# Moving the sums of the next weights, one weight buffer and twenty subtractions in a two-layer encoder trunk

## The chip, the cores and the metric

The kernel runs on one core of a Trainium2 chip. The metric is the device time of one execution in microseconds (us); the time before is the median of 3 runs, 2132.06 us (2131.26 to 2143.67). A core has TensorE for matrix products, VectorE, ScalarE and GpSimd for elementwise work, and a queue on SyncE (SP) that issues the transfers. Each engine works through its own instructions in order; they wait for one another through semaphores.

## The reference, cut to what matters

Two layers, each made of a feed-forward block, a mixer (dilated attention beside an mLSTM) and a second feed-forward block, each between two RMS norms. x is 512 tokens by 1024. The change touches the first half of the feed-forward block alone, four times in the program:

```python
def swiglu(h, w_in, w_out):
    gu = h @ w_in                      # 512 x 1024 times 1024 x 5632
    g, u = jnp.split(gu, 2, axis=-1)   # gate and up, 2816 columns each
    return (jax.nn.silu(g) * u) @ w_out
```

## The kernel before, in words

**Products.** Weights and activations are float32, but each product is made of three passes over rounded parts: a high part `hi` (a cast on ScalarE) and a low part `lo` (the source minus `hi`, a subtraction). TensorE runs hi by hi, hi by low and low by hi (`product`, L242 to L248: 12 matmuls of 256 columns for half of the 1024 rows).

**Blocks of the feed-forward input.** `ffn_in` (L252) cuts the 2816 gate columns, and the up columns with them, into 22 blocks f of 128. The first five, the **opening**, are made plainly (`block`, L273): for the left 256 tokens, then for the right 256. Each loads gate and up weights (512 KB each) into a ring of three buffers `raw`, casts `hi` (L97) and subtracts `lo` (L98). In the five left blocks the gate's `lo` is made on VectorE and the up's on GpSimd (`G if pool and gu`). While the left blocks run, the norm, transposes and splits of the last two token tiles are still being made (`post`, `pre`, `put`); the small power in `rsqrt_sum` (L135) runs on GpSimd, the rest on VectorE and ScalarE. In the first feed-forward block these are the first instructions of the program, and `first_gain` spreads the first norm's gain through a small product.

**The other 17 blocks** (`seven`, L333) use a scheme of seven products in place of eight for the two token halves and two row halves. Besides the gate weights g and up weights u it needs four sums of their halves, made by four VectorE additions (`Weights.sums`, L311 to L314) into `ws`, and their casts and low parts (L288, L290). A block's weights are prepared while the block before it runs: inside `seven`, the calls on `nxt` are written between the products. The order on TensorE, VectorE and ScalarE in there is the order of writing (`manual_schedule`); elsewhere the framework's scheduler sets it. The gate of the left tokens is the product `pa` copied (L343) plus the product `pb`, added on VectorE (L345), passed through silu on ScalarE (L348); then ScalarE copies `pa` out (L353), and TensorE may write `pa` again (the third use of that bank in the block).

**Buffers.** The gate weights of a block are loaded into the ring of three. The up weights go to `wu`, one of two buffers (slots 17 and 19 of `chunk`): block 5 in slot 19, block 6 in slot 17, and so on by turns. The same two slots hold `xf`, the float copy of the activations from which the scheme's combinations are made; the last reading of slot 17 is `xx.finish()` (L219, L220), just ahead of the 17 blocks. The transfers are issued on SP in an order that the scheduler sets.

Of the kernel before, what the change touches and what calls it, by code (L numbers as in the profile page):

```python
# [15 lines left out]
ALU = mybir.AluOpType  # L16
# [5 lines left out]
D = 1024  # L22
# [19 lines left out]
def trunk_kernel(ctx, tc, x, norm_gain, ffn_w_in, ffn_w_out, mix_w_in, conv_w, conv_b,  # L42
                 gate_bias, mlstm_norm_gain, mix_w_out, cst, out):
    nc = tc.nc
    V, A, G, PE = nc.vector, nc.scalar, nc.gpsimd, nc.tensor
# [19 lines left out]
    def chunk(name, slot, dt=F32):  # L65
        return big.tile([P, CH], dt, tag=f"slot{slot}", name=name, bufs=1)
# [17 lines left out]
    def t2(name, slot, dt=F32):  # L84
        return tp.tile([P, 516], dt, tag=f"t{slot}", name=name, bufs=1)
# [5 lines left out]
    def raw_tile():  # L91
        return wp.tile([P, 1056], F32, tag="raw", name="raw", bufs=3)

    def halves_of(src, n, sub=None):
        hi = wp.tile([P, 1056], F32R, tag="hi", name="hi", bufs=3)
        lo = wp.tile([P, 1056], F32R, tag="lo", name="lo", bufs=3)
        A.copy(hi[:, :n], src)  # L97
        (sub or V).tensor_tensor(lo[:, :n], src, hi[:, :n].bitcast(F32), ALU.subtract)  # L98
        return [[w[:, q: q + 512].rearrange("p (k c) -> p k c", k=4) for w in (hi, lo)] for q in range(0, n, 512)]
# [49 lines left out]
    def first_gain(g):  # L149
        row, one_row = chunk("row", 20)[0:1, :D], chunk("row", 21)[0:1, :P]  # L150
        nc.sync.dma_start(row, norm_gain[0, 0:1])
        G.memset(one_row, 1.0)
        for n in range(2):
            c = slice(n * 512, n * 512 + 512)
            ps = psB("gain")
            PE.matmul(ps, one_row, row[:, c], start=True, stop=True)
            A.mul(g[:, c], ps, math.sqrt(D))

    def post(t, banks, y):
        ss = small("post_ss", 2)  # L160
# [27 lines left out]
    def fp(ap):  # L188
        return ap.bitcast(F32)
# [62 lines left out]
    def ffn_in(layer, j, xx, late=None):  # L252
        w = ffn_w_in[layer, j].rearrange("(k p) c -> p k c", p=P)
        hts = [None] * NF
        left, right, both = slice(0, 256), slice(256, 512), slice(0, 512)
        sums = [0]

        def load(f, gu, pieces=1, whole_f=False):
            raw = chunk("wu", 17 + 2 * (f % 2)) if gu and not whole_f else raw_tile()
            col = gu * FF + f * P  # L260
            dst = raw[:, :1024].rearrange("p (k c) -> p k c", k=NK)
            for k in range(0, NK, NK // pieces):
                nc.sync.dma_start(dst[:, k: k + NK // pieces], w[:, k: k + NK // pieces, col: col + P])
            return raw

        def h_of(f):
            if f % 2 == 0:
                hts[f] = chunk("ht", f // 2)
                hts[f + 1] = hts[f][:, 512:1024]
                hts[f] = hts[f][:, 0:512]  # L270
            return hts[f]

        def block(f, c, pool=False, pieces=1):  # L273
            h = h_of(f) if hts[f] is None else hts[f]
            banks = []
            for gu in range(2):
                lo_k, hi_k = halves_of(load(f, gu, pieces, True)[:, :1024], 1024, G if pool and gu else None)
                ps = psA("gu")[:, c]
                for q, w2 in enumerate((lo_k, hi_k)):
                    product(ps, w2, [x[:, 4 * q: 4 * q + 4, c] for x in (xx.h, xx.l)], q == 0)  # L280
                banks.append(ps)
            sil = t2("sil", f % 2)[:, c]
            A.activation(sil, banks[0], AF.Silu)
            V.tensor_tensor(h[:, c], banks[1], sil, ALU.mult)

        def cast_pair(hi, lo, src):

            A.copy(hi, src)  # L288
            yield
            V.tensor_tensor(lo, src, fp(hi), ALU.subtract)  # L290
            yield [[x[:, q: q + 512].rearrange("p (k c) -> p k c", k=4) for x in (hi, lo)]
                   for q in range(0, src.shape[1], 512)]

        def ring():
            return [wp.tile([P, 1056], F32R, tag=q, name=q, bufs=3)[:, :1024] for q in ("hi", "lo")]

        class Weights:


            def __init__(self, f):  # L300
                self.g, self.u = load(f, 0), load(f, 1)

            def sums(self):
                out = []
                for q in range(2):
                    out.append(chunk("ws", (18, 20, 21)[sums[0] % 3])[:, :1024])
                    sums[0] += 1
                self.s12, self.s34 = out
                s1, s2, s3, s4 = [o[:, q: q + 512] for o in out for q in (0, 512)]
                g1, g2, u1, u2 = [w[:, q: q + 512] for w in (self.g, self.u) for q in (0, 512)]  # L310
                V.tensor_tensor(s1, u1, u2, ALU.add)  # L311
                V.tensor_tensor(s3, g1, u1, ALU.subtract)
                V.tensor_tensor(s2, s1, g1, ALU.subtract)
                V.tensor_tensor(s4, g2, s2, ALU.subtract)  # L314

            def raw(self):
                self.a = cast_pair(*ring(), self.g[:, :1024])
                next(self.a)

            def one(self):  # L320
                self.one_ = cast_pair(*ring(), self.s12)
                next(self.one_)

            def two(self):
                self.two_ = cast_pair(*ring(), self.s34)
                next(self.two_)

            def last(self):
                w = one.tile([P, D], F32R, tag="nt", name="a22", bufs=2)
                self.last_ = cast_pair(w[:, :512], w[:, 512:1024], self.u[:, 512:1024])  # L330
                next(self.last_)

        def seven(f, w, nxt):  # L333
            h = h_of(f) if hts[f] is None else hts[f]
            ps = (ps_even, ps_odd)[f % 2]
            ta, tb, tc_ = [t2(q, 3 * (f % 2) + n) for n, q in enumerate(("ha", "hb", "hc"))]
            a, b, c = [ps(q)[:, :256] for q in ("pa", "pb", "pc")]
            sil0, s1, u2, s5, g1, u1 = h[:, left], ta[:, left], ta[:, right], tb[:, left], tb[:, right], tc_[:, left]
            if nxt:
                nxt.sums()  # L340
            a11, a12 = w.a
            product(a, a11, xx.b11, True)
            A.copy(s1, a)  # L343
            product(b, a12, xx.b21, True)
            V.tensor_tensor(sil0, s1, b, ALU.add)  # L345
            if nxt:
                nxt.raw()
            A.activation(sil0, sil0, AF.Silu)  # L348
            if nxt:
                nxt.a = next(nxt.a)  # L350
            w1, w2 = w.one_
            product(a, w2, xx.t[2], False)
            A.copy(u2, a)  # L353
            product(c, w1, xx.t[1], True)
            if nxt:
                nxt.one()
            A.copy(s5, c)
            if nxt:
                nxt.last()
                nxt.one_ = next(nxt.one_)  # L360
            w3, w4 = w.two_
            product(a, w3, xx.t[3], False)
            V.tensor_tensor(u1, s5, a, ALU.add)
            if nxt:
                nxt.last_ = next(nxt.last_)
            product(c, w4, xx.b22, False)
            V.tensor_tensor(g1, u2, c, ALU.add)
            if nxt:
                nxt.two()
            A.activation(g1, g1, AF.Silu)  # L370
            if nxt:
                nxt.two_ = next(nxt.two_)
            product(a, w.last_[0], xx.t[4], False)
            V.tensor_tensor(h[:, left], a, sil0, ALU.mult)
            V.tensor_tensor(h[:, right], u1, g1, ALU.mult)

        ne = 5
        for f in range(ne):
            block(f, left, True, 2 if late and f == 0 else 1)
            if late and f < 2:  # L380
                late[f]()
        for f in range(ne):
            block(f, right)
        xx.finish()
        now = Weights(ne)
        now.sums()
        for q in (now.raw, now.one, now.two, now.last):
            q()
        now.a, now.one_, now.two_, now.last_ = [next(q) for q in (now.a, now.one_, now.two_, now.last_)]
        with tc.manual_schedule(engines={mybir.EngineType.PE, mybir.EngineType.DVE, mybir.EngineType.Activation}):  # L390
            for f in range(ne, NF):
                nxt = Weights(f + 1) if f + 1 < NF else None
                seven(f, now, nxt)
                now = nxt
        return hts
# [536 lines left out]
    late = [lambda: start(2), lambda: start(3)]  # L932
    for layer in range(DEPTH):
        for sub in range(3):
# [4 lines left out]
            else:  # L939
                halves = ffn_out(layer, sub // 2, ffn_in(layer, sub // 2, xx, late), last)  # L940
                late = None
# [52 lines left out]
```

## Time and profile before

| | |
|---|---|
| median of 3 runs | 2132.06 us |
| profiled execution, time | 2134.65 us |
| profiled execution, span | 2132.9 us |
| TensorE busy in the span | 2069.2 us (97%) |
| VectorE, ScalarE, GpSimd busy | 1532.7, 1135.7, 313.4 us |
| mean granted clock of TensorE | 0.992 |

The profiled execution took 2134.65 us, 1.8 us more than its span and 2.6 us more than the median of the runs. A sum made against it is carried over to the median by its difference. TensorE is busy nearly throughout, so the time is the clean length of its instructions and the gaps between them; the places to look at are the gaps, what ended each, and stretches in which the clock was lower.

### The profile page before, as it was taken

Reading aid. Unit: us, or ns where it says so; the run is one execution under the profiler, and the core shown is the slowest. Engines: PE = TensorE matmul, PEld = TensorE weight load, DVE = VectorE, ACT = ScalarE, POOL = GpSimd, SP = SyncE. Lnnn points to the kernel's source line nnn. Section 1 sums busy time; section 2 is a strip of 40 time slices with the busy share of each in tenths; the row PEclk is TensorE's granted clock in tenths of the full one; section 3 lists DMA queues with packets and bytes.
Section 4 is the critical chain, followed back from the end, with each engine's and each line's share of the span. In section 5 each row is a group of like instructions: output and inputs, shape, how many; then the busy total and the mean of one; then the engine's idle time right before and its main releaser. Section 6 shows DMA issues by size and latency. Waiting matters only on the chain.

```text
span 2132.9 us, 35684 instructions
## 1 busy us (share of the span) xinstructions
PE 2069.2 (97%) x13918; PEld 1859.1 (87%) x13918; DVE 1532.7 (72%) x2572; ACT 1135.7 (53%) x2036; POOL 313.4 (15%) x358
## 2 busy tenths in 40 slices
PE   7999999999999999999999999999999999999998
PEld 6999988889976899998899999888898679999886
DVE  6688757785666878875787886667756568788665
ACT  5455546545565645555654555554455555455554
POOL 3000001433522300000030000014334122000000
PEclk9999999999999999999999999999999999999999
DMA  6533355541112653335565333554411236433364
GB/s 190 165 106 107 101 185 189 156 118 54 59 51 89 188 158 100 102 99 187 186 188 149 100 105 122 188 187 139 119 40 41 75 122 177 123 109 109 113 206 147
DMA packets 305887, 274.49 MB, mean 129 GB/s; under 512 B 8789, under 2 KB 275509, under 8 KB 305718
## 3 DMA queue, kind: packets, MB, share of 16 engines
q1 hardware_dynamic: 305718, 272.21, 42.5%
q8 instruction: 109, 1.79, 0.4%
q14 instruction: 60, 0.49, 0.1%
HBM read 270.08 MB, written 2.10 MB: 128 GB/s over the span
## 4 chain that ended last, share of the span: by engine, by line
PE 84%; DVE 8%; DMA 3%; issue 3%; ACT 2%; POOL 0%; SPq 0%; DVEq 0%; POOLq 0%; ACTq 0%
PE o L409 9%; PE o L412 9%; PE o L410 9%; PE pa L246 6%; PE pa L247 6%; PE pa L248 6%; PE pc L246 3%; PE pc L248 3%; PE pc L247 3%; PE nat L493 3%; PE nat L494 3%; PE nat L495 3%; PE po L887 2%; PE pb L247 1%; PE pb L248 1%
## 5 line engine op out<-in xcount | busy, mean ns | idle before, releaser
L114 DVE TENSOR_TENSOR lo<-raw,hi 128x1024 fp32r<-128x1024 f32 (+1 forms) x272 | 338.0, 1243 | 228.0 <-ACT hi L113 227.5
L113 ACT CAST hi<-raw 128x1024 fp32r<-128x1024 f32 (+1 forms) x280 | 294.7, 1053 | 321.9 <-PE o L412 226.9
L290 DVE TENSOR_TENSOR lo<-ws,hi 128x1024 fp32r<-128x1024 f32 x136 | 166.6, 1225 | 111.6 <-ACT hi L288 111.6
L410 PE MATMUL o<-lo,hq 128*128 128x512 f32 x704 | 236.9, 394 | 0.8 <-DVE lo L114 0.8
L412 PE MATMUL o<-hi,hq 128*128 128x512 f32 x704 | 223.3, 394 | 0.0
L409 PE MATMUL o<-hi,hq 128*128 128x512 f32 x704 | 210.5, 395 | 2.5 <-ACT hq L446 2.5
L288 ACT CAST hi<-ws 128x1024 fp32r<-128x1024 f32 x136 | 142.9, 1051 | 123.3 <-PE pc L247 114.8
L493 PE MATMUL nat<-hi,xh 128*128 128x256 f32 (+1 forms) x640 | 187.2, 294 | 0.0
L248 PE MATMUL gu<-xh,lo 128*128 128x256 f32 x640 | 181.7, 286 | 4.3 <-DVE lo L98 3.7
L494 PE MATMUL nat<-lo,xh 128*128 128x256 f32 (+1 forms) x640 | 182.7, 286 | 2.5 <-DVE lo L114 2.3
L247 PE MATMUL gu<-xl,hi 128*128 128x256 f32 x640 | 181.8, 285 | 2.7 <-DVE xl L201 2.7
L246 PE MATMUL gu<-xh,hi 128*128 128x256 f32 x640 | 182.0, 286 | 0.4 <-ACT hi L97 0.4
L495 PE MATMUL nat<-hi,xl 128*128 128x256 f32 (+1 forms) x640 | 182.3, 286 | 0.0
L246 PE MATMUL pa<-tq,hi 128*128 128x256 f32 x544 | 154.4, 284 | 14.5 <-ACT ha L353 14.5
L409 PEld LDWEIGHTS o<-hi,hq 128*128 128x128 f32 x704 | 131.9, 188 | 34.0 <-ACT hq L446 3.4
L246 PE MATMUL pc<-xh,hi 128*128 128x256 f32 x544 | 160.5, 295 | 0.0
L410 PEld LDWEIGHTS o<-lo,hq 128*128 128x128 f32 x704 | 131.9, 188 | 31.4 <-DVE lo L114 1.1
L412 PEld LDWEIGHTS o<-hi,hq 128*128 128x128 f32 x704 | 132.2, 188 | 30.8
L247 PE MATMUL pa<-tq,hi 128*128 128x256 f32 x544 | 154.4, 284 | 0.0
L248 PE MATMUL pa<-tq,lo 128*128 128x256 f32 x544 | 154.3, 284 | 0.0
L248 PE MATMUL pc<-xh,lo 128*128 128x256 f32 x544 | 153.7, 282 | 0.0
L247 PE MATMUL pc<-xl,hi 128*128 128x256 f32 x544 | 153.7, 282 | 0.0
(237 smaller groups left out, 5679.3 us busy)
## 6 DMA issues: line engine op xcount, KB each, us to landing
raw<-in_ffn_w_out_dram SPq DMA_DIRECT2D x176, 512.0 KB, 3.5
raw<-in_ffn_w_in_dram SPq DMA_DIRECT2D x146, 512.0 KB, 4.0
wu<-in_ffn_w_in_dram SPq DMA_DIRECT2D x68, 512.0 KB, 3.9
raw<-in_mix_w_in_dram SPq DMA_DIRECT2D x56, 512.0 KB, 3.8
raw<-in_mix_w_out_dram SPq DMA_DIRECT2D x32, 512.0 KB, 3.8
raw<-in_mix_w_in_dram SPq DMA_DIRECT2D x16, 528.0 KB, 3.8
gpost<-in_norm_gain_dram SPq DMA_DIRECT2D x6, 512.0 KB, 5.8
gpre<-in_norm_gain_dram SPq DMA_DIRECT2D x5, 512.0 KB
```

Of the source, the lines that this page charges most:

```text
L113: A.copy(h, r)
L114: (sub or V).tensor_tensor(l, r, h.bitcast(F32), ALU.subtract)
L246: PE.matmul(ps, wh[:, k], xh[:, k], start=start and k == 0, stop=False, skip_group_check=True)
L247: PE.matmul(ps, wh[:, k], xl[:, k], start=False, stop=False, skip_group_check=True)
L248: PE.matmul(ps, wl[:, k], xh[:, k], start=False, stop=k == 3, skip_group_check=True)
L290: V.tensor_tensor(lo, src, fp(hi), ALU.subtract)
L409: PE.matmul(banks[t][n], a, wh[:, n], start=first, stop=False)
L410: PE.matmul(banks[t][n], a, wl[:, n], start=False, stop=False)
L412: PE.matmul(banks[t][n], b, wh[:, n], start=False, stop=end)
L493: PE.matmul(d, xh[:, k, tok], wh[:, k % 4], start=k == 0, stop=False)
L494: PE.matmul(d, xh[:, k, tok], wl[:, k % 4], start=False, stop=False)
L495: PE.matmul(d, xl[:, k, tok], wh[:, k % 4], start=False, stop=k == NK - 1)
```

## The change

Four edits, none of which changes what is computed:

- `first_gain`: the two scalings of the gain go from ScalarE to VectorE.
- `block`: the five left blocks make the up's low part on VectorE, as the gate's (20 subtractions in the program leave GpSimd).
- `Weights`: the up weights of block 6 (`ne + 1`) are loaded into the ring of three, not into slot 17. All other up weights stay in the two slots.
- `seven`: the four sums of the next weights are called behind the addition of the first gate (L345 before, L343 after), not ahead of the first product.

```diff
@@ first_gain
-            A.mul(g[:, c], ps, math.sqrt(D))
+            V.tensor_scalar(g[:, c], ps, math.sqrt(D), None, ALU.mult)
@@ block
-        def block(f, c, pool=False, pieces=1):
+        def block(f, c, pieces=1):
...
-                lo_k, hi_k = halves_of(load(f, gu, pieces, True)[:, :1024], 1024, G if pool and gu else None)
+                lo_k, hi_k = halves_of(load(f, gu, pieces, True)[:, :1024], 1024)
@@ Weights
-                self.g, self.u = load(f, 0), load(f, 1)
+                self.g, self.u = load(f, 0), load(f, 1, whole_f=f == ne + 1)
@@ seven
-            if nxt:
-                nxt.sums()
             a11, a12 = w.a
             product(a, a11, xx.b11, True)
             A.copy(s1, a)
             product(b, a12, xx.b21, True)
             V.tensor_tensor(sil0, s1, b, ALU.add)
             if nxt:
+                nxt.sums()
                 nxt.raw()
@@ end of ffn_in
-            block(f, left, True, 2 if late and f == 0 else 1)
+            block(f, left, 2 if late and f == 0 else 1)
```

How the instructions stand shows at three places. The first is VectorE at the start of the 17 blocks, in block 5 (`ws` are the sums, `lo<-ws,hi` the low parts of sums, `ht<-ha,pb` the first gate's addition). Before:

```order
L290 TENSOR_TENSOR lo<-ws,hi 128x1024
L220 TENSOR_TENSOR xl<-xf,xh 128x4x256
L284 TENSOR_TENSOR ht<-gu,sil 128x256
L290 TENSOR_TENSOR lo<-ws,hi 128x1024
L311 TENSOR_TENSOR ws<-wu 128x512
L312 TENSOR_TENSOR ws<-raw,wu 128x512
L313 TENSOR_TENSOR ws<-ws,raw 128x512
L314 TENSOR_TENSOR ws<-raw,ws 128x512
L345 TENSOR_TENSOR ht<-ha,pb 128x256
L290 TENSOR_TENSOR lo<-raw,hi 128x1024
```

With the change:

```order
L290 TENSOR_TENSOR lo<-ws,hi 128x1024
L220 TENSOR_TENSOR xl<-xf,xh 128x4x256
L284 TENSOR_TENSOR ht<-gu,sil 128x256
L290 TENSOR_TENSOR lo<-ws,hi 128x1024
L343 TENSOR_TENSOR ht<-ha,pb 128x256
L311 TENSOR_TENSOR ws<-raw 128x512
L312 TENSOR_TENSOR ws<-raw 128x512
L313 TENSOR_TENSOR ws<-ws,raw 128x512
L314 TENSOR_TENSOR ws<-raw,ws 128x512
L290 TENSOR_TENSOR lo<-raw,hi 128x1024
```

The first gate's addition moved ahead of the four sums, and these read block 6's up weights from `raw`. The blocks after it have the same order, with `wu`.

The second place is VectorE in the first opening, where the third token tile is split (`tr` is a transposed tile in PSUM, `t_269` to `t_271` and `tq` are the scheme's combinations of it). Before:

```order
L284 TENSOR_TENSOR ht<-gu,sil 128x256
L98 TENSOR_TENSOR lo<-raw,hi 128x1024
L201 TENSOR_TENSOR xl<-tr,xh 128x4x128 x2
L231 TENSOR_TENSOR xf<-tr,xf 128x4x128
L234 TENSOR_TENSOR t_269<-tr,xf 128x512
L235 TENSOR_TENSOR t_270<-tr,x_258 128x512
L236 TENSOR_TENSOR t_271<-xf,t_269 128x512
L201 TENSOR_TENSOR xl<-tr,xh 128x4x128 x2
L220 TENSOR_TENSOR tq<-t_269,tq 128x4x128
L220 TENSOR_TENSOR tq<-t_270,tq 128x4x128
L284 TENSOR_TENSOR ht<-gu,sil 128x256
L220 TENSOR_TENSOR tq<-t_271,tq 128x4x128
L98 TENSOR_TENSOR lo<-raw,hi 128x1024
```

With the change:

```order
L98 TENSOR_TENSOR lo<-raw,hi 128x1024
L284 TENSOR_TENSOR ht<-gu,sil 128x256
L98 TENSOR_TENSOR lo<-raw,hi 128x1024
L201 TENSOR_TENSOR xl<-tr,xh 128x4x128 x2
L231 TENSOR_TENSOR xf<-tr,xf 128x4x128
L234 TENSOR_TENSOR t_269<-tr,xf 128x512
L235 TENSOR_TENSOR t_270<-tr,x_258 128x512
L98 TENSOR_TENSOR lo<-raw,hi 128x1024
L236 TENSOR_TENSOR t_271<-xf,t_269 128x512
L220 TENSOR_TENSOR tq<-t_269,tq 128x4x128
L284 TENSOR_TENSOR ht<-gu,sil 128x256
L220 TENSOR_TENSOR tq<-t_270,tq 128x4x128
L98 TENSOR_TENSOR lo<-raw,hi 128x1024
```

The low parts of the up weights (L98) now stand in VectorE's queue between the splits, and block 3's gate low part, the last row of both, stands ahead of the last two `tq` and of the fourth tile's `xl`.

The third place is SP's queue in the first opening. Before:

```order
L263 DMA raw<-in_ffn_w_in_dram 128x8x128 x5
L263 DMA wu<-in_ffn_w_in_dram 128x8x128
L263 DMA raw<-in_ffn_w_in_dram 128x8x128 x11
L263 DMA wu<-in_ffn_w_in_dram 128x8x128
L263 DMA raw<-in_ffn_w_in_dram 128x8x128 x2
L263 DMA wu<-in_ffn_w_in_dram 128x8x128
```

With the change:

```order
L263 DMA raw<-in_ffn_w_in_dram 128x8x128 x7
L263 DMA wu<-in_ffn_w_in_dram 128x8x128
L263 DMA raw<-in_ffn_w_in_dram 128x8x128 x9
L263 DMA wu<-in_ffn_w_in_dram 128x8x128
L263 DMA raw<-in_ffn_w_in_dram 128x8x128 x2
L263 DMA wu<-in_ffn_w_in_dram 128x8x128
```

In both the second `wu` is block 7's. Before, the third `wu` is block 6's, behind the gates of blocks 7 and 8; now block 6's up weights are the first of the two `raw` that follow the second `wu`, and the third `wu` is block 8's.

## Rows read from the trace of the kernel before

**Rows 1.** Waits of TensorE, whole run: waited for, us in total, times, longest.

```profile
PE pa L246 <- ACT ha L353: 14.5, 4, 4.4
```

**Rows 2.** Stretches between first `pb`s: us; busy by engine; TensorE clock; DMA share; GB/s.

```profile
86.91:99.95 13.04, 10.22 (x87) 10.02 (x85) 9.38 (x14) 5.21 (x9) 0.00 (x0) 1.00 0.39 113
99.95:110.07 10.12, 10.12 (x87) 9.98 (x85) 8.35 (x14) 5.31 (x9) 0.00 (x0) 1.00 0.33 97
772.40:788.76 16.36, 12.54 (x86) 12.34 (x85) 9.51 (x14) 5.21 (x9) 0.00 (x0) 0.79 0.44 125
1136.96:1151.89 14.93, 11.48 (x87) 11.27 (x85) 9.49 (x15) 5.20 (x9) 0.00 (x0) 0.89 0.39 112
1824.49:1840.62 16.13, 11.72 (x86) 11.52 (x85) 9.45 (x14) 5.20 (x9) 0.00 (x0) 0.89 0.43 121
```

**Rows 3.** Timeline, first feed-forward block, block 5: start, us, engine, instruction [idle before].

```profile
80.11 2.48 SPq L263 DMA_DIRECT2D raw<-in_ffn_w_in_dram  x2
85.34 1.23 DVE L220 TENSOR_TENSOR xl<-xf,xh 128x1024 fp32r<-128x1024 f32 x1 [0.27 <-ACT xh L219]
86.60 0.37 SPq L263 DMA_DIRECT2D wu<-in_ffn_w_in_dram  x1
88.42 1.05 ACT L288 CAST hi<-raw 128x1024 fp32r<-128x1024 f32 x1 [0.94 <-PE pb L247]
90.44 0.69 DVE L311 TENSOR_TENSOR ws<-wu 128x512 f32<-128x512 f32 x1 [2.41 <-DMA wu<-in_ffn_w_in_dram]
92.98 0.41 DVE L345 TENSOR_TENSOR ht<-ha,pb 128x256 f32<-128x256 f32 x1
94.16 0.39 PE L246 MATMUL pa<-tq,hi 128*128 128x256 f32 x1 [2.82 <-ACT ha L353]
```

**Rows 4.** Stretches of the four openings, columns as in rows 2.

```profile
17.29:85.36 68.07, 63.66 (x496) 62.79 (x496) 47.35 (x61) 35.11 (x52) 12.93 (x8) 0.97 0.63 176
707.93:770.85 62.92, 59.67 (x496) 58.68 (x495) 52.15 (x77) 37.37 (x60) 14.47 (x11) 1.00 0.66 189
1074.35:1135.43 61.08, 59.29 (x496) 58.63 (x495) 52.31 (x77) 35.41 (x58) 16.78 (x11) 1.00 0.70 199
1760.05:1822.95 62.90, 59.50 (x497) 58.63 (x495) 52.20 (x77) 37.33 (x60) 13.14 (x10) 1.00 0.63 183
```

**Rows 5.** Costliest groups, GpSimd's and VectorE's low parts: busy us, mean ns | idle before.

```profile
L98 POOL TENSOR_TENSOR lo<-raw,hi 128x1024 fp32r<-128x1024 f32 x20 | 49.4, 2469 | 90.7 <-ACT hi L97 90.4
L98 DVE TENSOR_TENSOR lo<-raw,hi 128x1024 fp32r<-128x1024 f32 x60 | 77.8, 1299 | 21.9 <-ACT hi L97 21.6
```

**Rows 6.** Timeline of the first opening, around TensorE's gap there.

```profile
41.02 2.38 POOL L98 TENSOR_TENSOR lo<-raw,hi 128x1024 fp32r<-128x1024 f32 x1 [3.72 <-ACT hi L97]
41.11 3.37 DVE L98 TENSOR_TENSOR lo<-raw,hi 128x1024 fp32r<-128x1024 f32 x1
44.54 0.38 PE L248 MATMUL gu<-xh,lo 128*128 128x256 f32 x1 [3.09 <-DVE lo L98]
```

**Rows 7.** Timeline of a later block, 14, of the first feed-forward block.

```profile
181.15 0.68 DVE L311 TENSOR_TENSOR ws<-wu 128x512 f32<-128x512 f32 x1
182.52 1.05 ACT L288 CAST hi<-raw 128x1024 fp32r<-128x1024 f32 x1 [0.98 <-PE pb L247]
183.68 0.42 DVE L345 TENSOR_TENSOR ht<-ha,pb 128x256 f32<-128x256 f32 x1
184.01 1.22 DVE L290 TENSOR_TENSOR lo<-raw,hi 128x1024 fp32r<-128x1024 f32 x1
186.46 1.23 DVE L290 TENSOR_TENSOR lo<-ws,hi 128x1024 fp32r<-128x1024 f32 x1 [1.23 <-ACT hi L288]
187.60 0.41 DVE L363 TENSOR_TENSOR hc<-hb,pa 128x256 f32<-128x256 f32 x1
188.17 0.19 PEld L246 LDWEIGHTS pa<-tq,a 128*128 128x128 f32 x1
```

**Rows 8.** Timeline of the third opening, a power on GpSimd.

```profile
1083.99 0.99 POOL L135 TENSOR_TENSOR rs_yo<-rs_uo,mhalf 128x1 f32<-128x1 f32 x1 [2.44 <-DVE rs_uo L134]
```

## The prediction

> **What bounds the kernel now.** TensorE works nearly without a break, so I read the views in this order: TensorE's waits, the stretches in which they lie, the timeline of one such stretch, and then what else the change touches. The waits name a single place that is there once in each of the four feed-forward blocks and costs 14.5 us: `pa` waits for ScalarE's copy [rows 1]. The stretches from one first `pb` to the next show that it is block 5, the first of the 17: these four take 13.04, 16.36, 14.93 and 16.13 us, where the block behind the first of them takes 10.12 [rows 2]. The excess is 2.92 + 6.24 + 4.81 + 6.01 = 19.98 us. It has two parts, and the reader can take them apart in the same rows: TensorE's busy time there is 10.22 + 12.54 + 11.48 + 11.72 = 45.96 us, 5.48 more than 4 x 10.12; the rest, 14.5, is the wait. The 5.48 are matmuls that ran slower behind the gap: in three of the four stretches the granted clock is 0.79 to 0.89, and 1.00 in the one without a gap.
>
> The timeline says what the wait hangs on [rows 3]. Slot 17 is read for the last time by `xl` at 85.34. Only then is block 6's `wu` issued, at 86.60, and the first sum that reads it starts at 90.44, 3.84 later. The sums stand ahead of the first gate's addition in VectorE's queue, so that this addition, whose product `pb` was done about 88.5 (ScalarE's cast that it released starts at 88.42), starts at 92.98; silu and the copy of `pa` follow, and TensorE goes on at 94.16 after 2.82 us of nothing.
>
> The second place is the openings. They last 68.07, 62.92, 61.08 and 62.90 us, and weights are being loaded into TensorE for 62.79, 58.68, 58.63 and 58.63 of them [rows 4]. The differences, 5.28 + 4.24 + 2.45 + 4.27 = 16.24 us, are about what waits cost there. The largest is in the first opening: 3.09 us for a low part on VectorE [rows 6].
>
> **The change, part by part.**
>
> *Block 6's up weights in the ring, and the sums behind the addition.* The two go together. The ring's slot for them comes free with the last low part of the opening; before, the two `raw` transfers issued from 80.11 on took such slots [rows 3]. An issue near 80.1 and the 3.84 us of the `wu` row make it land near 84, 4 us before `pb` ends. The addition then starts at about 88.5 and silu behind the cast that ends at 88.42 + 1.05 = 89.5, so `pa` is copied by about 90.4, ahead of the 91.3 at which TensorE ran dry (94.16 - 2.82). The wait is gone, and with it what makes the clock drop: **-20.0**. Should the transfer come late, only the sums are late, and the first who needs them is the cast of the next block's second pair; the gate no longer stands behind it. Its bounds are -20.0 and, if another wait takes over at once, 0.
>
> *The sums in the 16 other blocks.* There TensorE has no gap, so the order can only cost. In block 14 [rows 7] `pb` ends about 182.55 and the addition starts at 183.68, behind the sums. Now it starts at 182.6; the sums (183.68 - 181.15 = 2.53 us) run from about 182.9 to 185.5, then the low part, 1.22, which before began at 184.01. VectorE had 1.23 us idle before 186.46, which takes up nearly all of the 1.45 by which this low part is later. The next low part starts at about 186.6 for 186.46, and `hc` ends near 188.15 for 188.01 (187.60 + 0.41). TensorE needs it at 188.17. With the few hundredths that a semaphore takes, this is a tie: 0 to 0.1 us in each of the 64 blocks, **+2**, bounds 0 and +6. ScalarE's later casts wait for TensorE, not for the sums, so they stay.
>
> *Twenty low parts from GpSimd to VectorE.* VectorE gets 20 x 1.22 = 24.4 us (1.22 is the undisturbed length in rows 7), and GpSimd loses 49.4 [rows 5]. What VectorE gets back: while GpSimd makes its low part, a VectorE subtraction takes 3.37 us, 2.15 more [rows 6]; the mean of VectorE's own L98 is 1.299 [rows 5]. If all 20 hold an instruction of VectorE that long, it gains 43; if 11 do, it comes out even. I take even: VectorE is as full in the openings as it was, 52 of 61 to 63 us in three of them [rows 4]. What changes is lateness. The low part of an up is done 1.22 us after its cast, not 2.47, its ring slot comes free as much earlier, and GpSimd's powers no longer queue behind a low part. Openings two to four wait for the normed tokens on VectorE, whose queue stays full: -1 each, of 4.24, 2.45 and 4.27. In the first, the late subtraction at 41.11 stood behind three `tq` and was then held to 3.37; with the change block 3's stands two instructions ahead of that and unhindered. At 41.45 TensorE needed it; by the lengths above it ends near 39, so the 3.09 go, and with them the slower matmuls behind the gap (the clock is 0.97 over this opening [rows 4]): -4.8 of 5.28. Together **-8**, bounds 0 and -16.2; below nothing, if VectorE's queue gets longer, see the rivals.
>
> Here a rule of the Trainium skill bears on the sum. The row shows the 3.37 for 1.22 while GpSimd reads two tiles. The page SBUF — State Buffer (section SBUF: two separate sides) says that VectorE with two SBUF inputs and GpSimd lock each other out of a shared port pair for a whole instruction; by that rule, and the row agrees, VectorE is freed here. But it speaks against the change as well, since the moved subtractions have two such inputs. By it, a power on GpSimd that comes just behind such a start is held for up to 1.22. The trace has a power of a single column that took 0.99 us [rows 8], which no run here yet explains. As a mechanism of this kernel it is the second rival below.
>
> *The gain's scaling.* The second half waited on ScalarE behind the norm of the second token tile; it now runs on VectorE ahead of the norm. VectorE also gets the second low part at the start, so that the next tile is hardly earlier: **-0.4**, between -1.5 and +1.
>
> Sum: -20.0 + 2 - 8 - 0.4 = -26.4 us against the profiled execution's 2134.65 us, so 2108. The median is 2.6 lower, so 2106; I put it at **2107**, because block 5 can give no more than its whole excess and may well fall a little short of it.
>
> **Rivals.**
>
> *The openings give nothing* (0.14). VectorE's queue, not GpSimd, sets them: it is busy 52 of 61 us, and each moved low part stands ahead of a split that someone waits for. For it speaks the fullness of VectorE in openings two to four. Against it: the gap of 3.09 us has a held subtraction as its direct cause. Time: 2132 - 20 + 2 = 2114, within 1%.
>
> *The powers are held* (0.04). Each opening's norms go VectorE, GpSimd's power, VectorE. If every power of the openings, four in each, is held by a low part for 1.22 us and the whole chain is late by it, that is 16 x 1.22 = 20 us: 2132 - 20 + 2 + 20 = 2134, no change. For it speaks the power of 0.99 us [rows 8]; against it that before such a power stood behind low parts of 2.47 on its own engine.
>
> *The block's tie is lost* (0.06). If `hc` is late by 0.15 us in each of 64 blocks, 10 us come back: 2116. This is the place from which the change could end slower: with x us per block beyond the tie, 64x is paid, and at x = 0.41 the 26 us are eaten; at 0.75 the kernel is at 2154. For x that large the low part would have to wait for something beside the sums; VectorE's 8.35 busy of 10.12 us [rows 2] leave 1.77 for it. **Slower than before**: 0.03.
>
> *The wait stays in another form* (0.05). The ring's slot for block 6's up weights comes free too late, or the transfer behind block 7's `wu` on SP is held. Then the sums, and the cast behind them, come late and half of the 20 us remain: 2132 - 10 - 6 = 2116.
>
> **How the numbers follow.** The forecast has 0.68, the rivals the rest. The range, 2096 to 2118, runs from all of the openings' 16 us and the whole of block 5's 20 (2132 - 36) to the case in which the openings give nothing and the tie costs 6. One per cent, about what a measurement of this kernel can tell from no change, is 21.3 us, or 2110.7. Of the forecast's cases some seven in eight lie below it, as its openings may give 3 us or 16: 0.59, and 0.01 from rivals that come out small, 0.60 together for faster; 0.03 for slower is the last case of the tie; 0.37 is left for within 1%.
>
> **What would show it.** In the trace after, the waits of TensorE should have no line `pa` on ScalarE's copy, and the four stretches of block 5 should be 10.1 to 10.3 us with clock 1.00. The first sum of block 6 should start behind the addition and wait for no transfer. The later blocks should stay at 10.10 to 10.20; at 10.3 or more the tie is lost. VectorE's L98 should have 80 instructions with a mean near 1.22, and no VectorE instruction of the openings should take twice its usual length. The first opening should be near 63 us, the others near 60 to 62. If they stay at 61 to 63, the first rival holds. The forecast is wrong in its main step if block 5 still takes over 12 us.

## The result and the profile after

The changed kernel takes **2105.95 us** (median of 4 runs, 2105.01 to 2107.81) against 2134.11 us of the kernel before on the same chip: a ratio of 0.9861, 95% interval [0.9829, 0.9894]. The forecast was 2107. Its profiled execution took 2105.01 us, with a span of 2103.3 us and a mean granted clock of 0.996. Ratios leave out three runs at a much lower clock (2254.79 us of the kernel before, 2424.16 of the gain alone, 2843.16 of the sums ahead).

TensorE's waits no longer have a line `pa` on ScalarE's copy, the line of [rows 1]. What is left at the head of the list is the start of the program and the norms; in the 17 blocks a single wait is listed:

```profile
PE tr L182 <- DVE nt L178: 9.2, 4, 5.0
PE pc L246 <- ACT hb L356: 0.2, 1, 0.2
```

The stretches from one first `pb` to the next answer to [rows 2] (same columns: us, then busy time of TensorE, of its weight loads, VectorE, ScalarE and GpSimd, then TensorE's clock). Block 5 of the four feed-forward blocks is rows one, three, four and five, the block behind the first of them row two:

```profile
79.47:89.72 10.25, 10.25 (x87) 10.08 (x86) 9.32 (x15) 5.32 (x9) 0.00 (x0) 1.00 0.47 133
89.72:99.96 10.24, 10.24 (x87) 10.04 (x86) 8.37 (x14) 5.32 (x9) 0.00 (x0) 1.00 0.36 105
760.05:770.29 10.24, 10.24 (x86) 10.08 (x85) 9.30 (x14) 5.32 (x9) 0.00 (x0) 1.00 0.48 140
1119.36:1129.73 10.37, 10.19 (x87) 9.98 (x85) 9.28 (x15) 5.32 (x9) 0.00 (x0) 1.00 0.51 140
1799.29:1809.53 10.24, 10.24 (x87) 10.09 (x85) 9.30 (x14) 5.33 (x9) 0.00 (x0) 1.00 0.50 143
```

Two things are to be seen. Block 5 fell from 60.46 to 41.1 us in all, at clock 1.00 throughout. And the later block is not at 10.12 as before but at 10.24. The openings, answering to [rows 4], in the same columns:

```profile
17.56:77.93 60.37, 60.37 (x496) 60.14 (x496) 45.24 (x64) 33.94 (x49) 2.89 (x4) 1.00 0.69 193
700.12:758.51 58.39, 58.39 (x497) 58.39 (x495) 50.56 (x82) 37.33 (x59) 7.51 (x6) 1.00 0.74 209
1057.51:1117.83 60.32, 58.93 (x496) 58.50 (x495) 52.06 (x81) 36.48 (x58) 5.44 (x6) 1.00 0.71 201
1739.34:1797.75 58.41, 58.41 (x496) 58.41 (x495) 50.49 (x82) 37.32 (x59) 5.32 (x5) 1.00 0.70 199
```

In three of the four, TensorE's busy time is the whole stretch. VectorE's busy time did not grow though it took over twenty low parts: 50.56 us for 52.15 in the second. The group of its low parts, of [rows 5], shows a small part of why (most lies on other instructions, of which the part on the openings tells below); it has 80 members now, at 1.222 us for 1.299, which is 4.6 us over the 60 of before:

```profile
L98 DVE TENSOR_TENSOR lo<-raw,hi 128x1024 fp32r<-128x1024 f32 x80 | 97.8, 1222 | 23.3 <-ACT hi L97 22.8
```

Block 5's VectorE, where [rows 3] had the first sum wait 2.41 us for its transfer. The addition L343 starts as soon as `pb` is done, and the first sum follows with no wait:

```profile
81.17 0.42 DVE L343 TENSOR_TENSOR ht<-ha,pb 128x256 f32<-128x256 f32 x1 [0.57 <-PE pb L248]
81.51 0.69 DVE L311 TENSOR_TENSOR ws<-raw 128x512 f32<-128x512 f32 x1
```

Block 14, as in [rows 7], is where the price is. First VectorE and ScalarE, then TensorE's weight loads:

```profile
186.59 1.22 DVE L290 TENSOR_TENSOR lo<-raw,hi 128x1024 fp32r<-128x1024 f32 x1
187.72 1.22 DVE L290 TENSOR_TENSOR lo<-ws,hi 128x1024 fp32r<-128x1024 f32 x1
188.86 0.41 DVE L362 TENSOR_TENSOR hc<-hb,pa 128x256 f32<-128x256 f32 x1
...
186.40 1.05 ACT L288 CAST hi<-ws 128x1024 fp32r<-128x1024 f32 x1 [0.97 <-PE pc L247]
187.36 0.36 ACT L356 COPY hb<-pc 128x256 f32<-128x256 f32 x1
...
187.45 0.19 PEld L248 LDWEIGHTS pa<-tq,lo 128*128 128x128 f32 x1
187.77 0.19 PEld L246 LDWEIGHTS pc<-xh,hi 128*128 128x128 f32 x1
...
189.07 0.19 PEld L248 LDWEIGHTS pc<-xh,lo 128*128 128x128 f32 x1
189.33 0.19 PEld L246 LDWEIGHTS pa<-tq,a 128*128 128x128 f32 x1
```

Loads otherwise follow one another every 0.12 us, at all but two places. Between the last two rows lie 0.26, and this place is new: `pa<-tq,a` writes the bank that the addition of `hc` reads, and that ends at 189.27. It stands behind two low parts without a gap between them, so each tenth by which the sums end later reaches TensorE. The other place is `pc<-xh,hi`, 0.32 behind the load in front of it and just behind ScalarE's copy of `pc` (187.36 + 0.36). The kernel before has it too, with 0.33:

```profile
186.33 0.37 ACT L357 COPY hb<-pc 128x256 f32<-128x256 f32 x1
186.42 0.19 PEld L248 LDWEIGHTS pa<-tq,lo 128*128 128x128 f32 x1
186.75 0.19 PEld L246 LDWEIGHTS pc<-xh,hi 128*128 128x128 f32 x1
```

Where all of it went, in us. The columns are the start (up to the first gate product), the four openings as in [rows 4], block 5 four times, the 15 periods behind block 5 in each of the four feed-forward blocks, and all the rest of the span. Each kernel is one profiled execution, and line numbers are each kernel's own; the experiments follow below.

| kernel | span | start | openings | block 5 | 60 other periods | rest |
|---|---|---|---|---|---|---|
| before | 2132.9 | 17.3 | 68.1 + 62.9 + 61.1 + 62.9 = 255.0 | 60.5 | 607.7 | 1192.5 |
| changed | 2103.3 | 17.6 | 60.4 + 58.4 + 60.3 + 58.4 = 237.5 | 41.1 | 614.1 | 1193.0 |
| before, ring alone | 2126.5 | 17.5 | 255.1 | 54.1 | 607.6 | 1192.1 |
| before, sums alone | 2130.0 | 16.6 | 254.7 | 51.5 | 614.1 | 1193.0 |
| before, low parts alone | 2118.2 | 16.4 | 62.2 + 58.4 + 60.3 + 58.4 = 239.3 | 61.9 | 607.6 | 1192.9 |
| before, gain alone | 2130.9 | 18.4 | 62.9 + 62.2 + 60.9 + 62.2 = 248.2 | 63.4 | 608.2 | 1192.7 |
| changed, sums ahead | 2109.9 | 17.5 | 237.7 | 54.4 | 607.6 | 1192.8 |
| changed, sums behind in block 5 alone | 2096.8 | 16.7 | 237.7 | 40.9 | 607.6 | 1193.9 |
| changed, subtractions on GpSimd | 2128.4 | 19.6 | 62.2 + 64.8 + 68.2 + 65.1 = 260.2 | 41.3 | 614.6 | 1192.8 |
| changed, fills on GpSimd | 2113.8 | 16.7 | 60.3 + 61.9 + 60.4 + 61.9 = 244.6 | 41.3 | 614.6 | 1196.6 |
| changed, copy of `pc` first | 2086.9 | 17.9 | 238.4 | 39.8 | 596.6 | 1194.2 |
| changed, both | 2085.5 | 17.1 | 238.1 | 39.8 | 596.7 | 1193.8 |

From before to changed that is +0.3 - 17.5 - 19.4 + 6.4 + 0.5 = -29.7 us. The table is read by columns: an edit shows in its own column, and the last one says that little moved elsewhere (within 2 us, but for the run with the fills, where some 3.6 us lie that I did not follow).

### The profile page after: what moved, and what is told of

Read it like the earlier page. It is cut to its first block, busy times and chain, and to the rows that moved or that the text cites. A ratio compares the mean times of both kernels' runs of the same rounds, so it can differ in the third digit from the quotient of the medians.

```text
span 2103.3 us, 35628 instructions
## 1 busy us (share of the span) xinstructions
PE 2065.3 (98%) x13918; PEld 1854.0 (88%) x13918; DVE 1529.3 (73%) x2594; ACT 1136.1 (54%) x2034; POOL 269.8 (13%) x338
```

## The experiments

**The ring alone** (the kernel before with this one line):

```diff
-                self.g, self.u = load(f, 0), load(f, 1)
+                self.g, self.u = load(f, 0), load(f, 1, whole_f=f == ne + 1)
```

> The kernel before with one edit alone: block 6's up weights in the ring of three; the sums stay ahead of the first product. Theory (it was the late transfer that held the first gate): the sums wait for nothing, run from about 88.0 to 90.6 in the first feed-forward block, the gate's addition ends near 91.0, and TensorE waits for the copy of the first gate's bank by some 0.5 us instead of 2.8 to 4.4. Block 5 takes about 10.5 us in each of the four, the time falls by 18 us (15 to 20), and the other 64 blocks stay at 10.12. Rival (the order of the sums is what counts, and the slot little): block 5 stays over 12 us, and the time falls by less than 8.

Measured: 2126.25 us, ratio 0.9947 [0.9927, 0.9967], some 11 us and not 18, and by the profiled execution, 2 us slower than the median, 6.4; block 5 takes 13.0 to 13.8 us. Here the rival was right and my theory wrong. VectorE in block 5 of this run, and the stretch in the columns of [rows 2]:

```profile
86.06 0.69 DVE L311 TENSOR_TENSOR ws<-raw 128x512 f32<-128x512 f32 x1 [2.79 <-DMA raw<-in_ffn_w_in_dram]
86.67 1.22 DVE L290 TENSOR_TENSOR lo<-ws,hi 128x1024 fp32r<-128x1024 f32 x1
...
89.13 1.22 DVE L220 TENSOR_TENSOR xl<-xf,xh 128x1024 fp32r<-128x1024 f32 x1
...
91.73 0.69 DVE L314 TENSOR_TENSOR ws<-raw,ws 128x512 f32<-128x512 f32 x1
92.34 0.42 DVE L345 TENSOR_TENSOR ht<-ha,pb 128x256 f32<-128x256 f32 x1
...
86.97:100.73 13.76, 11.93 (x87) 11.51 (x86) 11.17 (x16) 5.21 (x9) 0.00 (x0) 0.88 0.42 120
```

In the kernel before the sums stood behind the last `xl` in the queue, since that reading freed the slot of their weights. With the slot out of the way the scheduler set three of them ahead of `xl`, and VectorE now waits at the first for the transfer, with `xl` and the gate behind it. The gate's addition starts at 92.34, hardly earlier than the 92.98 of [rows 3], and TensorE's waits have two new lines in place of one:

```profile
PE pa L246 <- ACT ha L353: 6.2, 4, 1.5
PE pc L247 <- DVE xl L220: 3.0, 4, 0.9
```

**The sums alone** (the kernel before, `nxt.sums()` moved, slot 17 kept):

```diff
-            if nxt:
-                nxt.sums()
             a11, a12 = w.a
...
             if nxt:
+                nxt.sums()
                 nxt.raw()
```

> The kernel before with one edit alone: the sums behind the first gate's addition; block 6's up weights stay in slot 17. Theory (late transfer): the gate is free, but the sums still start when the transfer lands, near 90.4, and the cast of the first sum pair, the copy of pc behind it on ScalarE and the low parts come late; block 5 keeps some 1.5 to 2 us of its excess in each of the four (6 to 10 in all of 20), and the 64 other blocks cost 0.1 us each, 6.4: the time changes by -6 (-9 to 0). Rival (order alone does it): block 5 falls to 10.3 us and the time by 13. Second rival (the other blocks were not slowed by the order of the sums but by something else of the change): they stay at 10.12 here and the time falls by 10 to 14.

Measured: 2129.99 us, ratio 0.9971 [0.9957, 0.9985], 6 us as expected. The gate is free (its addition starts at 86.95), but the sum after it waits for the transfer, the cast of the first pair for the sum, and behind that cast on ScalarE stands the copy that TensorE needs:

```profile
88.61 0.69 DVE L311 TENSOR_TENSOR ws<-wu 128x512 f32<-128x512 f32 x1 [1.25 <-DMA wu<-in_ffn_w_in_dram]
...
PE pc L246 <- ACT hb L356: 7.7, 4, 2.6
```

Block 5 keeps 11.0 us of its excess, where 6 to 10 were expected. So of its 19.4 us one edit alone brings 6.4 and the other 9.0 in the profiled executions. With neither alone is block 5 down to the 10.2 to 10.4 us of the changed kernel (13.0 to 13.8, and 11.6 to 13.9). Whether the two together bring more than their sum stays open: by the ratios the ring alone brings some 11 us and the sums alone, without their price in the other periods, some 12.6. The 60 other periods cost 6.4 here too, so that price belongs to the order of the sums.

**The low parts alone** (the kernel before, the up's `lo` of the left blocks on VectorE):

```diff
-                lo_k, hi_k = halves_of(load(f, gu, pieces, True)[:, :1024], 1024, G if pool and gu else None)
+                lo_k, hi_k = halves_of(load(f, gu, pieces, True)[:, :1024], 1024)
```

> The kernel before with one edit alone: the twenty low parts on VectorE. Theory (GpSimd's low parts came late and held VectorE): the four openings are 60.4, 58.4, 60.3 and 58.4 us as in the kernel with all edits, and the time falls by 17 us (13 to 19). Rival (the openings were shortened by another of the edits, or their gain is paid back in block 5): under 6 us.

Measured: 2119.89 us, ratio 0.9923 [0.9904, 0.9942], 16 us; the openings are within 0.1 us of the changed kernel's but for the first, 62.2 for 60.4. The openings' gain belongs to this edit.

**The gain's scaling alone** (the kernel before):

```diff
-            A.mul(g[:, c], ps, math.sqrt(D))
+            V.tensor_scalar(g[:, c], ps, math.sqrt(D), None, ALU.mult)
```

> The kernel before with one edit alone: the scalings of the gain on VectorE. Theory: it moves a start of 17.3 us by 0.3 at most, in either direction, and the time by -1 to +1. Rival (the first opening's gain of 7.7 us has its start in it): the time falls by 2 us or more.

Measured: 2133.43 us, ratio 0.9986 [0.9973, 0.9998], some 3 us (0.4 to 5.8), about the rival's number. But the table says otherwise than the rival: the start is 1.1 us later, and the first opening 5.2 us shorter, because the new order of its instructions no longer has the gap of 3.09 us [rows 6]; 2.9 come back in block 5, at a lower clock and with waits as before (14.7 us for 14.5), in this one execution. From the low parts alone, which remove that gap themselves, to the changed kernel, start and first opening go from 16.4 + 62.2 to 17.6 + 60.4, by some -0.7 us; the changed kernel has the ring and the sums too, so that this is not the gain's edit by itself.

**Sums ahead again, everywhere** (the changed kernel with the diff of the second experiment undone):

> The changed kernel with the sums ahead of the first product in every block, block 5 too; block 6's up weights stay in the ring. Theory from the run with the ring alone (once they wait for no transfer, the scheduler sets three of the four sums ahead of the last xl and the fourth ahead of the gate's addition, so that xl and the gate are late): block 5 takes 13 to 13.8 us in each of the four, the others 10.12, and the time is 5 to 8 us above the changed kernel. Rival (the late gate of that run came from the openings, whose low parts are now early): block 5 near 10.5, and the time 5 us under the changed kernel.

Measured: 2106.21 us (2105.71 to 2111.64, three runs), ratio 0.9887 [0.9858, 0.9916]. These times lie across those of the changed kernel, so they do not show the 5 to 8 us of the theory; the columns of the profiled executions do (6.6 us by the spans). Block 5 takes 54.4 us in all (12.2 to 15.4 each, a wider spread than the theory had), the other periods 607.6. The early opening does not help, since the sums are early with it:

```profile
78.34 0.69 DVE L311 TENSOR_TENSOR ws<-raw 128x512 f32<-128x512 f32 x1 [2.76 <-DMA raw<-in_ffn_w_in_dram]
...
81.41 1.22 DVE L220 TENSOR_TENSOR xl<-xf,xh 128x1024 fp32r<-128x1024 f32 x1
```

The transfer lands at 78.3, ahead of the 81.2 at which the changed kernel's gate takes VectorE, and still `xl` starts at 81.41 where the changed kernel has it at 77.91: it needs neither the transfer nor the sums, but it stands in the queue behind three sums, and the first of them waits for the landing. What the order of the sums gives in block 5, 13.3 us, is twice what it costs elsewhere.

**Sums behind the addition in block 5 alone**:

```diff
+            if nxt and f > ne:
+                nxt.sums()
             a11, a12 = w.a
...
             if nxt:
-                nxt.sums()
+                if f == ne:
+                    nxt.sums()
                 nxt.raw()
```

> The changed kernel with the sums behind the first gate's addition in block 5 alone, and ahead of the first product again in the later blocks. Theory (the 64 later blocks pay 0.10 us each for VectorE's later queue, and block 5 alone needs the new place): the later blocks go back from 10.24 to 10.12, block 5 stays at 10.3, and the time is 6.4 us under the changed kernel (5 to 7). Rival (the price lies elsewhere, in the clock or the transfers): no difference to the changed kernel, within 2 us. Second rival (block 6's early sums run into the late transfer of block 7's up weights): the first blocks behind block 5 grow by 0.5 us or more in each of the four.

Measured: **2098.55 us**, ratio 0.9836 [0.9818, 0.9854], 7.4 us under the changed kernel's median. The later periods are back at 607.6 and block 5 stays at 40.9.

**Work on GpSimd that nobody waits for** (the changed kernel; `spare` is a tile that is written and not read):

```diff
+        if sub is not None:
+            four = lambda t: t[:, :1024].rearrange("p (k c) -> p k c", k=4)
+            G.tensor_tensor(four(sub), idj.unsqueeze(1).to_broadcast([P, 4, 256]), four(hi).bitcast(F32), ALU.subtract)
...
-                lo_k, hi_k = halves_of(load(f, gu, pieces, True)[:, :1024], 1024)
+                lo_k, hi_k = halves_of(load(f, gu, pieces, True)[:, :1024], 1024, spare if gu else None)
```

> The changed kernel with work added on GpSimd that nobody waits for: beside each of the twenty left up blocks a subtraction of the same size (128 x 1024, two inputs in SBUF), written to a tile that is not read; VectorE keeps all low parts. Theory (hold: GpSimd's low parts lengthened VectorE's instructions, and that cost half or more of the openings' 17.5 us): VectorE's instructions beside them grow again by some 26 us in all, and the openings are 8 us or more longer than in the changed kernel. Rival (lateness: the low part of 2.47 us and its place in GpSimd's queue made the up weights late, the hold was covered): the openings stay within 3 us of the changed kernel's 238 us in all, though VectorE's instructions grow.

Measured: 2130.21 us, ratio 0.9981 [0.9971, 0.9991]; the openings take 260.2 us, 22.7 more than in the changed kernel and more than before the change. Counted from the trace, 19 of VectorE's instructions beside the added ones are longer than the shortest of their kind (held, in what follows), by 29.2 us together. In the second opening, GpSimd's subtraction and VectorE behind a low part:

```profile
715.42 3.08 POOL L101 TENSOR_TENSOR spare<-idj,hi 128x1024 f32<-128x1024 f32 x1
...
715.00 1.23 DVE L98 TENSOR_TENSOR lo<-raw,hi 128x1024 fp32r<-128x1024 f32 x1
716.15 2.37 DVE L141 SCALAR_TENSOR_TENSOR rs_yi<-rs_ai,rs_yi 128x1 f32<-128x1 f32 x1
...
719.69 0.55 PE L185 MATMUL tr<-idj,nt 128*128 128x128 f32 x3 [0.73 <-DVE nt L181]
```

L141 works on one column. It ends at 718.52, within 0.02 us of GpSimd's end at 718.50, the normed token tile is late by it, and TensorE stands 0.73 us at the transposes.

**Fills on GpSimd instead** (as before, but in the place of `G.tensor_tensor`):

```diff
+            G.tensor_copy(sub[:, :1], hi[:, :1].bitcast(F32))
+            for _ in range(3):
+                G.memset(sub[:, :1024], 0.0)
```

> The changed kernel with other work on GpSimd in the same twenty places: three fills of a tile of 128 x 1024 with zeros behind a copy of one column of the high part, so that GpSimd is busy but reads next to nothing. It tells apart the two ways in which the subtractions of the run with idle work on GpSimd cost 22.7 us in the openings. Theory (hold: VectorE's instructions are held while GpSimd reads two tiles): the fills hold nothing, VectorE's lengthening stays under 5 us, and the openings are 238 to 242 us in all. Rival (the powers queue behind the added work on GpSimd): the openings are 10 us or more longer than in the changed kernel, with the waits at the transposes behind the powers, and VectorE's instructions of usual length. Should the fills hold VectorE as well, both grow and the run decides nothing between them.

Measured: 2114.96 us, ratio 0.9916 [0.9888, 0.9943]. GpSimd is busy 72.2 us with it, more than the 59.5 of the subtractions, and holds two of VectorE's instructions, by 0.8 us in all (at both, a tensor-by-scalar product of GpSimd's own ran as well). The same kind of step of the norm on one column, within the time of the second of two fills, takes 0.16 us:

```profile
712.07 1.97 POOL L102 MEMSET spare<- 128x1024 f32 x2
...
713.74 0.16 DVE L142 SCALAR_TENSOR_TENSOR rs_yo<-rs_ao,rs_yo 128x1 f32<-128x1 f32 x1
```

The openings still grew by 7.1 us, all of it in the second and fourth: there a power stands behind three fills, and TensorE waits 1.67 us for the normed tile:

```profile
720.64 2.98 POOL L102 MEMSET spare<- 128x1024 f32 x3
723.58 0.55 POOL L139 TENSOR_TENSOR rs_yi<-rs_ui,mhalf 128x1 f32<-128x1 f32 x1
...
727.03 0.66 PE L186 MATMUL tr<-idj,nt 128*128 128x128 f32 x4 [1.67 <-DVE nt L182]
```

Neither theory's number was met (238 to 242 us, or 10 us more than the changed kernel); both have their part: of the 22.7 us some 7 are the queue in front of the powers, and the other 15 or so come with the two tiles that GpSimd reads. The split is an estimate, as the two runs do not queue alike.

**The copy of `pc` first** (the changed kernel):

```diff
-            if nxt:
-                nxt.one()
             A.copy(s5, c)
             if nxt:
+                nxt.one()
                 nxt.last()
-                nxt.one_ = next(nxt.one_)
...
             V.tensor_tensor(u1, s5, a, ALU.add)
             if nxt:
+                nxt.one_ = next(nxt.one_)
                 nxt.last_ = next(nxt.last_)
```

> The changed kernel with two neighbours swapped in each of the 17 blocks: ScalarE copies pc out ahead of the cast of the next block's first sum pair, and VectorE's addition of hc stands ahead of that pair's low part. Theory (in each block TensorE waits twice, about 0.1 us for the copy of pc and 0.15 us for hc, both behind preparation for the next block): the blocks fall from 10.24 to about 9.97, and the time by 15 to 18 us under the changed kernel. Rival (the preparation is as tight as the gate: the casts that come 0.4 us later make the next block's products wait): within 3 us of the changed kernel, or slower.

Measured: **2088.38 us**, ratio 0.9787 [0.9770, 0.9804], 17.6 us under the changed kernel. Every block takes 9.92 to 9.96 us. In block 14 the copy (L354) now runs ahead of the cast, and the addition of `hc` (L360) waits for TensorE, not TensorE for it:

```profile
184.60 0.37 ACT L354 COPY hb<-pc 128x256 f32<-128x256 f32 x1 [1.05 <-PE pc L248]
184.87 1.06 ACT L288 CAST hi<-ws 128x1024 fp32r<-128x1024 f32 x1
...
186.09 0.42 DVE L360 TENSOR_TENSOR hc<-hb,pa 128x256 f32<-128x256 f32 x1 [0.16 <-PE pa L248]
186.42 1.22 DVE L290 TENSOR_TENSOR lo<-ws,hi 128x1024 fp32r<-128x1024 f32 x1
```

**Both** (this swap and the sums behind the addition in block 5 alone):

> The swap of the run before and the sums ahead of the first product in all blocks but block 5, together. Theory (one and the same wait, for hc, is paid in both): no more than 2 us better than the swap alone. Rival (two separate waits): the two gains add, 20 us or more under the changed kernel.

Measured: **2087.65 us**, ratio 0.9781 [0.9765, 0.9797], the fastest of all, though not to be told from the swap alone. The 60 periods take 596.7 us for 596.6: once `hc` stands ahead of the low part, where the sums stand is free. So the price of the change in the later blocks is the wait for `hc`. The 0.17 us by which these blocks are shorter than those of the kernel before (10.12 for 9.95) are the other wait, for the copy of `pc`: in block 14 of the run with the swap alone its load comes 0.11 us behind the one in front, no longer 0.33. The run with the sums behind the addition in block 5 alone has that wait still and the one for `hc` not, so the table takes the two apart: of the swap's 17.5 us in the 60 periods 6.4 are `hc` (614.1 to 607.6) and 10.9 the copy of `pc` (607.6 to 596.7).

## Why the prediction came out right

**Block 5, -20.0.** Measured -19.4, by the mechanism that was forecast: transfer early, sums behind the addition, no gap, clock 1.00. Most of the missing 0.6 is the new period of 10.24, which block 5 also pays. The working has the clock at 1.00 only without a gap; but block 5 of the first feed-forward block had one, of 2.82 us [rows 3], and kept 1.00 [rows 2], so what a gap costs beyond its own length differs from block to block. That both edits are needed was said without a reason that held. For a late transfer I wrote that only the sums would then be late and nobody who matters behind them; the run of the sums alone shows TensorE waiting 7.7 us for the copy behind their cast.

**The tie, +2 (0 to +6).** Measured +6.4 over 60 of the 64 blocks, just over the upper bound: this term was mis-sized. The wait is the one named, for `hc`; each period lost 0.11 us, and 10.24 lies between the 10.20 and the 10.3 that were named as signs. The addition of the working went wrong by hundredths that it did not count: I let the addition start 0.05 us behind `pb`. In block 14 the addition starts 0.11 behind `pb`'s end (183.72 for 183.61), and the second low part at 187.72 where 186.6 was reckoned for a block with the addition at 182.6: 4.0 us behind the addition's start in both, so the length of the queue was right, and its start was late by a few hundredths that the tie had not to give: the load behind the one at 189.07 comes 0.14 us later than its usual 0.12. The rival of the lost tie, with 0.15 us, was nearer than the forecast's 0.03.

**The openings, -8 (0 to -16.2).** Measured -17.5, outside the bounds: the largest miss. The step that failed is "What changes is lateness", at -1 for each of the openings two to four; they gave -4.5, -0.8 and -4.5. In the second and fourth TensorE waited for the normed tokens most of all, 2.2 and 2.1 us, and not for an up's low part. The working had that wait, but took it to stay, since VectorE's queue stays full; with the change no wait is listed there. The second, before:

```profile
PE tr L182 <- DVE nt L178: 2.2, 2, 1.6
PE gu L247 <- DVE xl L201: 0.7, 1, 0.7
```

The account of VectorE's time itself was right. Counted from the trace of before, 16 instructions beside GpSimd's low parts were held, by 27.5 us together, against 24.4 added: even, as taken. But two thirds of the 27.5, 18.2 us, lay on three kinds of norm steps (L134, L137 and L169), of which two are one column wide and stand in the chain to the normed tokens that TensorE waits for. Two of them, with the hold in their length, as they stand in the chain that ended last in the trace of before:

```profile
718.74 2.15 DVE rs_uo L134
733.21 2.37 DVE rs_ai L137
```

The moved subtractions take about the same time in other places; that they cost less there is what the openings show, and no run took it apart. The experiment with idle work on GpSimd returns the loss and more, though no weights are made on GpSimd; by the fills, some 7 us of its 22.7 are powers that queue, which is a lateness that the prediction had named. The rule of the Trainium skill that the prediction weighed (SBUF — State Buffer, section SBUF: two separate sides) allows this: of a VectorE operation with two SBUF inputs and a GpSimd operation that reads SBUF, whichever starts first has the shared port pair for its whole instruction, and the other waits. The trace agrees, with 2.37 us for a step of 0.16 that ended within 0.02 us of GpSimd's; and with fills, which read nothing, and copies of one column, 0.8 us of holding in 72.2. I had used the rule for the long subtractions and not for the short steps. The third opening gave little because TensorE waits 0.8 and 0.6 us there at other places; VectorE is still held in it, by GpSimd's scaling of the norm gains (L147: an `xs` of 1.57 us for 0.74, a `tq` of 1.53 for 0.68), which may be why, but is not shown to be. So the sign that no VectorE instruction of the openings takes twice its usual length did not come: five do, all beside L147.

The first opening gave -7.7 for -4.8: beside the gap of 3.09 and what VectorE's `xl` cost, its slow matmuls are gone, TensorE's busy time falling from 63.66 to 60.37 us. And the bound of 16.2 was taken from weight-load time, which is itself longer where matmuls are slow (62.79 of [rows 4] became 60.14), so it was no bound.

**The gain, -0.4.** Beside the low parts, with the ring and the sums, some -0.7; alone about -3, through an order of instructions that no sum of durations shows.

**The rivals.** "The openings give nothing" and "the wait stays in another form" did not occur; the latter did with either of the two edits alone, as the runs show. Powers were held, one in each feed-forward block (1.46 to 1.58 us for 0.55, beside a low part on VectorE), but not four in each and not at a price that shows: in the second and fourth opening TensorE waits for nothing.

The errors partly met: -9.5 in the openings, +4.4 in the tie, +0.6 in block 5, +0.7 at the start and +0.5 elsewhere leave -3.3 against the sum of -26.4. That the forecast lies so near owes something to that.

## What to carry to other kernels

When work moves off an engine that held another one up, do not weigh busy time against busy time alone: look at which instructions were held, since a one-column step in a chain that someone waits for passes its whole delay on. Before calling a place in a queue a tie, list who stands between it and the engine that matters, and move that one ahead; here two such swaps were worth 17.6 us, most of it from a wait of 0.2 us a block that was there before and that the list of waits of the kernel before does not show. Look at the spacing of an engine's instructions, not only at its list of waits. And a freed buffer also frees the scheduler: work that no longer waits may be set ahead of what was early only because of that wait.

## What was not expected of the hardware

VectorE was held by GpSimd on 16 of the 48 instructions that overlapped with a low part, and on 2 of the 124 beside fills and one-column copies. A fill of 128 x 1024 took 0.955 us, and a copy of one column in front of it 0.75 us on average, from 0.18 to 1.24. Behind a gap the clock did not always fall: block 5 of the first feed-forward block waited 2.82 us and kept 1.00 in the kernel before, while the other three fell to 0.79 to 0.89 [rows 2], and in the run with the ring alone the same block fell to 0.88 behind waits of 0.31 and 1.53 us. What decides it no run here tells.
